# RWKV chunk recurrence in 64x64 quarters of TensorE's array, in a one-core hybrid layer

## The chip, the core and the metric

The kernel runs on one core of a Trainium2 chip. The metric is the device time of one execution in microseconds: the median of the runs shown, lower is better. [...]

## What is computed

One layer of a diffusion backbone over 512 latent tokens and 256 context tokens of width 2048: a modulated RMS norm, one input projection, an mLSTM head group and an RWKV-7 head group, an output projection, and a gated convolutional FFN. The change touches the RWKV group alone: 16 heads of 64 channels, scanned forward and backward, first over the context (from a zero state), then over the latent tokens (from the context's final state).

```python
def rwkv7_scan(r, w, k, v, kk, a, s0, reverse):
    def step(s, xs):
        r_t, w_t, k_t, v_t, kk_t, a_t = xs
        s = (s * w_t[:, :, None, :]
             - jnp.einsum("bhvk,bhk->bhv", s, kk_t)[..., None] * (kk_t * a_t)[:, :, None, :]
             + v_t[..., :, None] * k_t[..., None, :])
        return s, jnp.einsum("bhvk,bhk->bhv", s, r_t)
    ...
y = y_f + y_b
```

## The kernel before

All arithmetic is float32. The large projections split weights and operands in a high and a low part (lines 299 and 300) and make three products of each (lines 370 to 372 and 403 to 405). The RWKV scan is done in chunks of 64 tokens, 4 of context and 8 of latent tokens, for 8 pairs of heads and two directions. A pair and direction is a unit; two heads share the 128 partitions.

- prep makes a unit's operands: scaled keys and receptances KR, scaled b and k in BK, their products G (line 745), masked by VectorE (line 747), and the token-major b and k by transposes (line 756, copied by ScalarE in line 758). All goes to DRAM, to GK_d.
- tsolve inverts the 32x32 diagonal blocks of all chunks, a problem to a partition, in 60 operations of VectorE for a batch (lines 800 and 801), and stores the blocks (803 to 808).
- chain_load loads two chunks of a unit and joins the two inverted blocks to a 64x64 inverse, by eight 32x32 products into the tile ct (lines 834 and 838) and a copy by ScalarE (836) and by VectorE (839).
- chain_step does one chunk of one unit in the PSUM tile R: line 859 multiplies the state M, a block-diagonal [128, 128] of two heads, by the operands; 861 adds the values' part, a head at a time; ScalarE copies (863); 865 applies the inverse; ScalarE copies (866); 868 makes the state's update, 871 adds to y; ScalarE copies y (872); VectorE updates M (876), a head at a time.
- y of each unit is stored to DRAM, and finalize_pair loads both directions' and adds them (924). The state at the context's end goes through DRAM, Mst.

The jobs form a pipeline: operands of job i, inverses of job i - 1, chain of job i - 2 (x_job, ctx_job). In between stand the projections of the latent tokens, and VectorE accumulates late chunks of the modulation (232). A planner, which simulates times of its own, sets each engine's fixed order from the program's order and a few priorities (weight loads are drawn ahead by AHEAD). PSUM has eight banks: two acc, two pre, one ct, three R. SyncE's queue is in order: an issue that waits holds up those behind.

## Time and profile before

| | before |
|---|---|
| median of 3 runs, us | 3351.02 (3346.22 to 3354.89) |
| span of the profiled execution, us | 3344.3 |
| TensorE, VectorE, ScalarE busy | 97%, 63%, 36% |
| instructions | 50011 |
| mean rate of the DMAs | 165 GB/s |

The profile records one execution. An engine's busy time is the time in which it worked on an instruction; matmuls are pipelined and their ends are modelled, so a burst's own pace is read from the starts in order of time. In all views L and a number is a line of the kernel, and a tile is named without its buffer's number. Stages are given in us from the span's start.

### The profile page before, as it was taken

What the parts mean: (1) busy time and instruction counts of PE and PEld (TensorE: products, weight loads), DVE (VectorE), ACT (ScalarE), POOL (GpSimd) and SP (SyncE); (2) the same over time, 40 slices, a digit from 0 to 9 for tenths busy, and PEclk for the clock granted to TensorE, in tenths of its full rate; (3) what the DMA queues carried; (4) which work ended last, traced back from release to release, by engine and by line L of the source; (5) the groups of instructions that cost most, each with busy time, mean ns of one, the idle gap of its engine ahead of it and who ended that gap; (6) DMA issues with size and microseconds to landing.
All of it is one profiled execution on the core that took longest, in us unless ns stands there. A gap on an engine that the chain in (4) does not pass through costs nothing.

```text
span 3344.3 us, 50011 instructions
## 1 busy us (share of the span) xinstructions
PE 3246.0 (97%) x18566; PEld 2610.8 (78%) x18566; DVE 2097.5 (63%) x4010; ACT 1197.9 (36%) x2474; POOL 51.0 (2%) x113
## 2 busy tenths in 40 slices
PE   8999999999999999999998899999999999999998
PEld 5688778787787878777677688888888888888887
DVE  2578777777475776665754787465555555555657
ACT  4356544333334444344323432232222222222323
POOL 0000101000000000000000000000000000000000
PEclk9999999999999999999999999999999999999999
DMA  8878656566567678776764355333333333333332
GB/s 280 306 241 243 185 156 161 162 212 206 187 188 230 194 234 253 207 233 214 260 211 130 99 190 183 95 95 97 96 97 95 95 100 96 95 95 95 101 95 101
DMA packets 391938, 552.97 MB, mean 165 GB/s; under 512 B 131312, under 2 KB 256520, under 8 KB 391440
## 3 DMA queue, kind: packets, MB, share of 16 engines
q1 hardware_dynamic: 382048, 536.41, 51.9%
q10 hardware_dynamic: 9648, 13.37, 1.1%
q8 instruction: 147, 2.41, 0.3%
q14 instruction: 95, 0.78, 0.1%
HBM read 459.06 MB, written 90.61 MB: 164 GB/s over the span
## 4 chain that ended last, share of the span: by engine, by line
PE 82%; DMA 8%; DVE 6%; ACT 2%; issue 1%; SPq 1%; DVEq 0%; ACTq 0%
PE acc L372 12%; PE acc L371 12%; PE acc L370 12%; PE acc L1350 5%; PE acc L1351 5%; PE acc L1352 5%; DMA am<-in_wmod 3%; PE R L859 2%; PE R L861 2%; PE R L865 2%; PE pre L195 2%; PE acc L405 2%; PE acc L404 2%; PE pre L745 2%; PE acc L403 2%
## 5 line engine op out<-in xcount | busy, mean ns | idle before, releaser
L299 ACT CAST whi<-wraw 128x512 fp32r<-128x512 f32 (+1 forms) x948 | 569.7, 604 | 1319.8 <-PE acc L371 715.9
L300 DVE TENSOR_TENSOR wlo<-wraw,whi 128x512 fp32r<-128x512 f32 (+1 forms) x948 | 629.2, 666 | 457.5 <-ACT whi L299 440.6
L370 PE MATMUL acc<-H,whi 128*128 128x512 f32 x1920 | 761.7, 397 | 4.0 <-ACT ev L520 3.0
L372 PE MATMUL acc<-H,wlo 128*128 128x512 f32 x1920 | 761.4, 397 | 3.7 <-DVE wlo L300 3.7
L371 PE MATMUL acc<-H,whi 128*128 128x512 f32 x1920 | 761.1, 396 | 0.0
L372 PEld LDWEIGHTS acc<-H,wlo 128*128 128x128 f32 x1920 | 362.7, 189 | 83.8 <-DVE wlo L300 4.9
L370 PEld LDWEIGHTS acc<-H,whi 128*128 128x128 f32 x1920 | 362.9, 189 | 82.8 <-ACT ev L520 3.2
L371 PEld LDWEIGHTS acc<-H,whi 128*128 128x128 f32 x1920 | 362.8, 189 | 79.2 <-issue 3.6
L1354 DVE SCALAR_TENSOR_TENSOR x<-acc,mod,x 128x512 f32<-128x512 f32 (+1 forms) x192 | 135.6, 706 | 221.9 <-PE acc L1352 221.8
L1298 DVE SCALAR_TENSOR_TENSOR f_cv<-upad,fvec,f_cv 128x512 f32<-128x512 f32 x352 | 263.7, 749 | 7.2
L1350 PE MATMUL acc<-fh,whi 128*128 128x512 f32 x640 | 253.2, 396 | 0.0
L1351 PE MATMUL acc<-fl,whi 128*128 128x512 f32 x640 | 253.1, 396 | 0.0
L1352 PE MATMUL acc<-fh,wlo 128*128 128x512 f32 x640 | 253.1, 396 | 0.0
L232 DVE SCALAR_TENSOR_TENSOR adacc<-am,csil,adacc 128x512 f32<-128x512 f32 x240 | 179.4, 748 | 91.8 <-DMA am<-in_wmod 89.8
L404 PE MATMUL acc<-whi,H 128*128 128x256 f32 x512 | 155.7, 304 | 0.0
L403 PE MATMUL acc<-whi,H 128*128 128x256 f32 x512 | 154.6, 302 | 0.3 <-DVE ev L434 0.3
L405 PE MATMUL acc<-wlo,H 128*128 128x256 f32 x512 | 152.7, 299 | 0.3 <-DVE wlo L300 0.3
L1352 PEld LDWEIGHTS acc<-fh,wlo 128*128 128x128 f32 x640 | 120.2, 188 | 29.1
L1350 PEld LDWEIGHTS acc<-fh,whi 128*128 128x128 f32 x640 | 120.2, 188 | 29.0
L1351 PEld LDWEIGHTS acc<-fl,whi 128*128 128x128 f32 x640 | 120.2, 188 | 29.0
L876 DVE SCALAR_TENSOR_TENSOR r_M<-r_M,r_gC,R 64x64 f32<-64x64 f32 x352 | 98.3, 279 | 48.1 <-ACT r_yt L872 33.0
L1236 PE MATMUL acc<-H,whi 128*128 128x512 f32 x256 | 101.6, 401 | 9.0 <-ACT H L299 7.9
(346 smaller groups left out, 4837.3 us busy)
## 6 DMA issues: line engine op xcount, KB each, us to landing
am<-in_wmod SPq DMA_DIRECT2D x128, 512.0 KB
wraw<-in_wup SPq DMA_DIRECT2D x88, 512.0 KB
wraw<-in_wgate SPq DMA_DIRECT2D x88, 512.0 KB
wraw<-in_wdn SPq DMA_DIRECT2D x88, 512.0 KB
wraw<-in_wcm SPq DMA_DIRECT2D x72, 512.0 KB
r_GK<-GK_d SPq DMA_DIRECT2D x64, 512.0 KB
wraw<-in_wtm SPq DMA_DIRECT2D x56, 512.0 KB
GK_d<-r_Gp SPq DMA_DIRECT2D x32, 512.0 KB
```

What stands on the lines that cost most here:

```text
L299: act.copy(hi, t)
L300: dve.tensor_tensor(lo, t, hi.bitcast(F32), ALU.subtract)
L370: pe.matmul(pt[:, :n], hi(k8), H.h(k), start=k == 0, stop=False)
L371: pe.matmul(pt[:, :n], hi(k8), H.l(k), start=False, stop=False)
L372: pe.matmul(pt[:, :n], lo(k8), H.h(k), start=False, stop=k == KT - 1)
L403: pe.matmul(o, H.h(k)[:, xs], hi(k4), start=first, stop=False, skip_group_check=True)
L404: pe.matmul(o, H.l(k)[:, xs], hi(k4), start=False, stop=False, skip_group_check=True)
L405: pe.matmul(o, H.h(k)[:, xs], lo(k4), start=False, stop=k == KT - 1, skip_group_check=True)
L1298: dve.scalar_tensor_tensor(cv, u[:, a:a + GH, b:b + GW], fvec[:, f, tap:tap + 1], cv, ALU.mult, ALU.add)
L1350: pe.matmul(pt, hi(m)[:, k, :], th[:, cs], start=k == 0, stop=False)
L1351: pe.matmul(pt, hi(m)[:, k, :], tl[:, cs], start=False, stop=False)
L1352: pe.matmul(pt, lo(m)[:, k, :], th[:, cs], start=False, stop=k == GF - 1)
```

## The change

The recurrence holds each head on its own half of the partitions and works in 64x64 quarters of the array: a quarter reads partitions 0 to 63 or 64 to 127 and writes one of the two halves of a PSUM bank. Both directions of a pair are done in one step, in two banks of R, one for each head; a chunk's operands lie in one row of 512 floats (kc = 128 of KR, 2 kc of G, 128 of token-major b and k; 320 in context), in S_d. The backward direction's keys are stored in reversed order, so that both directions' systems are solved in the same form, without the transposed copies. The joins move from chain_load into tsolve, for all chunks of a pair at once, in the PSUM tile pre; the solved and joined rows go back to S_d. The state M, [128, 64] for a unit, stays on chip from context to latent tokens (16 buffers); v is loaded once for a pair; y of both directions is summed on chip by VectorE and stored once for a pair. R gets four banks, ct goes; the finalization's transposes use pre. The mask's table is made to suit. Comments are dropped throughout.

```diff
-    PB = {"acc": 2, "pre": 2, "ct": 1, "R": 3}
+    PB = {"acc": 2, "pre": 2, "R": 4}
...
-            dve.tensor_tensor(KR[:, cc, 0:64], v3(s.kk[:, 0:n]), E1[:, cc, e_prev], ALU.mult)
+            back = slice(None, None, -1) if d else slice(None)
+            dve.tensor_tensor(KR[:, cc, 0:64][:, :, back], v3(s.kk[:, 0:n]), E1[:, cc, e_prev], ALU.mult)
+            dve.scalar_tensor_tensor(BK[:, cc, 0:64][:, :, back], v3(t1)[:, cc], -1.0, v3(E2)[:, cc], ALU.mult, ALU.mult)
             if x:
                 dve.tensor_tensor(KR[:, cc, 64:128], v3(s.r), E1[:, cc, e_cur], ALU.mult)
-        dve.scalar_tensor_tensor(BK[:, :, 0:64], v3(t1), -1.0, v3(E2), ALU.mult, ALU.mult)
         dve.tensor_tensor(BK[:, :, 64:128], v3(kd), v3(E2), ALU.mult)
-        GK_d = DT("GK_d", [P, 2, 8, 256], 16)
-        G_d = GK_d[:, 0].rearrange("p c (h t) -> p c h t", t=128)
-        KB_d = GK_d[:, 1]
-        sp.dma_start(KB_d[:, :, 0:kc], KR[:, :, 0:kc])
-        # G^T[(b|k) s, (kappa|r) t] per chunk and head
+        sp.dma_start(S[:, :, 0:kc], KR[:, :, 0:kc])
         for hf in range(2):
-            G = rp("r_Gp", [P, 4, 2, 128], GPB)
+            G = rp("r_Gp", [P, 4, 2, kc], GPB)
             gd = d if x else hf
             pgs = [PS("pre", [P, 4, 128]) for _ in range(2)]
             for c4 in range(4):
                 for h, pg in enumerate(pgs):
-                    hs = slice(64 * h, 64 * h + 64)
+                    hs = LOHI[h]
                     c = 4 * hf + c4
                     pe.matmul(pg[:, c4, 0:kc], BK[hs, c, :], KR[hs, c, 0:kc], start=True, stop=True)
             for h, pg in enumerate(pgs):
-                dve.tensor_tensor(G[:, :, h, 0:kc], pg[:, :, 0:kc], gmask[:, gd, None, 0:kc].to_broadcast([P, 4, kc]), ALU.mult)
-            sp.dma_start(G_d[:, 4 * hf:4 * hf + 4, :, 0:kc], G[:, :, :, 0:kc])
-        # (b|k) e^(cum_C - cum), token-major, for the state
+                for j, js in enumerate(LOHI):
+                    dve.tensor_tensor(G[LOHI[h], :, j, :], pg[js, :, 0:kc], gmask[js, gd, None, 0:kc].to_broadcast([64, 4, kc]), ALU.mult)
+            sp.dma_start(S[:, 4 * hf:4 * hf + 4, kc:3 * kc], G.rearrange("p c j t -> p c (j t)"))
...
-            act.copy(bt, pb)
-            sp.dma_start(KB_d[:, cs, kc:kc + 128], bt)
+            for h, hs in enumerate(LOHI):
+                for js in LOHI:
+                    act.copy(bt[hs, :, js], pb[js, :, hs])
+            sp.dma_start(S[:, cs, 3 * kc:3 * kc + 128], bt)
...
+    def tsolve(pairs):
+        nc_ = 2 * pairs[0][0].nch
+        n = 4 * nc_ * len(pairs)
+        x = rp("t_X", [P, 32, 32], 1)[0:n]
+        def blocks():
+            q = 0
+            for us in pairs:
+                for r in range(0, P, 32):
+                    o = us[0].kc + r % 64
+                    yield x[q:q + nc_], us[0].S_d[r:r + 32, :, o:o + 32].rearrange("s c t -> c s t")
+                    q += nc_
...
-        dve.tensor_copy(X[half:n], Y[half:n].rearrange("p s t -> p t s"))
...
-        act.copy(Y, x.rearrange("p s t -> p t s"))
-        sp.dma_start(so[0, 0:n], X)
-        sp.dma_start(so[1, 0:n], Y)
-        for u in units:
-            for b in range(2):
-                for ps_, g in blocks(u, b):
-                    sp.dma_start(g, (X if u.d == 0 else Y)[ps_])
+        for t, g in blocks():
+            sp.dma_start(g, t)
+        XT = rp("t_X", [P, 2, 16, 32], 1)
+        for k, us in enumerate(pairs):
+            kc = us[0].kc
+            T_d = us[0].S_d[:, :, kc:kc + 64]
+            T = rp("t_Y", [P, 16, 64], 1)[:, 0:nc_]
+            sp.dma_start(T, T_d)
+            W = XT[:, k, 0:nc_]
+            dve.transpose(W, T[:, :, 0:32])
+            ws = [PS("pre", [P, 16, 32])[:, 0:nc_] for _ in range(2)]
+            a_, b_ = ([slice(64 * h + o, 64 * h + o + 32) for h in range(2)] for o in (0, 32))
+            f = dict(start=True, stop=True, skip_group_check=True)
+            for c in range(nc_):
+                for h, pw in enumerate(ws):
+                    pe.matmul(pw[b_[h], c, :], T[a_[h], c, 32:64], W[a_[h], c, :], **f)
+            for h, pw in enumerate(ws):
+                act.copy(W[b_[h]], pw[b_[h]])
+            for c in range(nc_):
+                for h, pw in enumerate(ws):
+                    pe.matmul(pw[a_[h], c, :], W[b_[h], c, :], T[b_[h], c, 32:64], **f)
+            for h, pw in enumerate(ws):
+                dve.tensor_copy(T[a_[h], :, 32:64], pw[a_[h]])
+            sp.dma_start(T_d, T)
...
+        o = rk("r_GK", [P, 2, 512], 6)[:, :, 0:3 * u.kc + 128]
+        sp.dma_start(o, u.S_d[:, cu:cu + 2, :])
...
+    def chain_v(p, seg, nch):
+        t = rk("r_V", [P, 8, 64], 3)[:, 0:nch]
+        for h, hs in enumerate(LOHI):
+            o = (p % 2) * 128 + 64 * h
+            sp.dma_start(t[hs], v_d[seg][p // 2, :, :, o:o + 64].rearrange("a (b t) v -> t (a b) v", t=64))
+        return t
...
+    def chain_step(us, ops, cs, V, y, first, last):
+        x = us[0].seg == "x"
+        kc = us[0].kc
+        bank = [PS("R", [P, 8, 64]) for _ in range(2)]
+        pos = (0, 1) if cs[0] < cs[1] else (1, 0)
+        opened = {}
+        def mm(h, half, o, w, rhs):
+            hs = LOHI[h]
+            out = bank[h][LOHI[half], o, :]
+            at = opened.get((h, half))
+            f = dict(stop=True, skip_group_check=True)
+            if at is None:
+                opened[(h, half)] = pe.matmul(out, w[hs], rhs[hs], start=True, **f)
+                return
+            with tc.issue_after(at.ins):
+                pe.matmul(out, w[hs], rhs[hs], start=False, **f)
+        w = [o[:, c % 2] for o, c in zip(ops, cs)]
+        kinds = range(2) if x else range(1)
+        for src in range(2):
+            for k, u in enumerate(us):
+                for j in kinds:
+                    for h in range(2):
+                        o = 2 * kc * src + 64 * j
+                        mm(h, h if j == 0 else 1 - h, pos[k], w[k][:, o:o + 64], u.M if src == 0 else V[:, cs[k], :])
+        Rs = rk("r_Rs", [P, 2, 64], 3)
+        U = rk("r_U", [P, 2, 64], 3)
+        for h, hs in enumerate(LOHI):
+            act.copy(Rs[hs], bank[h][hs, 0:2, :])
+        for k, u in enumerate(us):
+            for h in range(2):
+                mm(h, 1 - h, 2 + pos[k], w[k][:, kc:kc + 64], Rs[:, pos[k], :])
+            for h in range(2):
+                if not last:
+                    mm(h, h, 2 + pos[k], w[k][:, 3 * kc + 64:3 * kc + 128], V[:, cs[k], :])
+        for h, hs in enumerate(LOHI):
+            act.copy(U[hs], bank[h][LOHI[1 - h], 2:4, :])
+        for k, u in enumerate(us):
+            for h in range(2):
+                if not last:
+                    mm(h, h, 2 + pos[k], w[k][:, 3 * kc:3 * kc + 64], U[:, pos[k], :])
+            for h in range(2):
+                if x:
+                    mm(h, 1 - h, pos[k], w[k][:, kc + 64:kc + 128], U[:, pos[k], :])
+        if not last:
+            for k, u in enumerate(us):
+                g = u.g0 + cs[k]
+                for h, hs in enumerate(LOHI):
+                    dve.scalar_tensor_tensor(u.M[hs], u.M[hs], u.gC[hs, g:g + 1], bank[h][hs, 2 + pos[k], :], ALU.mult, ALU.add)
         if x:
+            lo, hi = min(cs), max(cs)
+            for h in range(2):
+                hs = LOHI[1 - h]
+                out = y[hs, lo:hi + 1:hi - lo, :]
+                if first:
+                    dve.tensor_copy(out, bank[h][hs, 0:2, :])
+                else:
+                    dve.tensor_tensor(out, bank[h][hs, 0:2, :], out, ALU.add)
+    def chain(pairs, mid):
+        x = pairs[0][0].seg == "x"
+        nch = pairs[0][0].nch
+        Vs, ys = [], []
+        for us in pairs:
+            Vs.append(chain_v(us[0].p, us[0].seg, nch))
+            ys.append(rk("r_yt", [P, 8, 64], 2) if x else None)
+            for u in us:
+                if not x:
+                    Mst[(u.p, u.d)] = rk("r_M", [P, 64], 16)
+                    pool.memset(Mst[(u.p, u.d)], 0.0)
+                u.M = Mst[(u.p, u.d)]
+        n = nch // 2
         for i in range(n):
+            if x and i == 1:
                 mid()
+            ops = [[chain_load(u, i if u.d == 0 else n - 1 - i) for u in us] for us in pairs]
+            for c in range(2 * i, 2 * i + 2):
+                for us, o, V, y in zip(pairs, ops, Vs, ys):
+                    chain_step(us, o, (c, nch - 1 - c), V, y, c < nch // 2, x and c == nch - 1)
+        if x:
+            for us, y in zip(pairs, ys):
+                y_d = us[0].y_d = DT("yr_d", [4, P, 128], 8)
+                for h in range(2):
+                    sp.dma_start(y_d[:, :, 64 * h:64 * h + 64].rearrange("a (b t) v -> t (a b) v", t=64), y[LOHI[1 - h]])
...
-        for t, u in ((y, uf), (sq, ub)):
-            sp.dma_start(t, u.y_d.rearrange("a p v -> p a v"))
+        sp.dma_start(y, uf.y_d.rearrange("a p v -> p a v"))
         g4 = lambda t: t.rearrange("p a (h c) -> p (a h) c", h=2)
         b8 = lambda t: t[:, :, None].to_broadcast([P, 8, 64])
-        dve.tensor_tensor(y, y, sq, ALU.add)
```

## Rows read from the trace of the kernel before

**Rows 1.** The page: span, busy time by engine, chain that ended last.
```profile
span 3344.3 us, 50011 instructions
...
PE 3246.0 (97%) x18566; PEld 2610.8 (78%) x18566; DVE 2097.5 (63%) x4010; ACT 1197.9 (36%) x2474; POOL 51.0 (2%) x113
...
PE 82%; DMA 8%; DVE 6%; ACT 2%; issue 1%; SPq 1%; DVEq 0%; ACTq 0%
```
**Rows 2.** Busy time by stage: busy us (instructions) by engine, granted clock, DMA share, GB/s.
```profile
400.00:1650.00 1250.00, 1222.26 (x8721) 964.31 (x8722) 836.70 (x1911) 503.47 (x1252) 27.97 (x71) 0.97 0.69 206
200.00:400.00 200.00, 186.75 (x1258) 166.16 (x1256) 167.28 (x325) 122.37 (x209) 20.19 (x19) 0.98 0.73 220
500.00:600.00 100.00, 99.17 (x810) 78.79 (x809) 74.76 (x196) 41.05 (x98) 9.98 (x11) 0.98 0.58 159
```
**Rows 3.** The same view, from 400 to 1650 us, for tile R, then ct.
```profile
400.00:1650.00 1250.00, 353.56 (x2782) 263.31 (x2782) 98.27 (x352) 127.27 (x512) 0.97 0.69 206
...
400.00:1650.00 1250.00, 91.22 (x1560) 66.63 (x1560) 31.38 (x102) 24.35 (x96) 0.97 0.69 206
```
**Rows 4.** TensorE in order of time (start, length, line, shapes, count): chunks' bursts.
```profile
1012.61 0.49 PE L859 MATMUL R<-r_M,r_GK 128*128 128x128 f32 x2
1012.93 0.39 PE L868 MATMUL R<-r_UV,r_GK 128*128 128x128 f32 x2
1013.25 0.45 PE L871 MATMUL R<-r_UV,r_GK 128*64 128x64 f32 x4
1013.63 0.44 PE L861 MATMUL R<-r_UV,r_GK 64*64 64x64 f32 x4
1014.00 0.71 PE L745 MATMUL pre<-r_KR,r_BK 64*128 64x128 f32 x4
```
**Rows 5.** The same view: the dense stream, a burst of the recurrence, the stream again.
```profile
1015.22 0.28 PE L404 MATMUL acc<-whi,H 128*128 128x256 f32 x1
1015.33 0.28 PE L405 MATMUL acc<-wlo,H 128*128 128x256 f32 x1
1015.54 0.45 PE L871 MATMUL R<-r_UV,r_GK 128*64 128x64 f32 x4
1015.92 0.39 PE L403 MATMUL acc<-whi,H 128*128 128x256 f32 x1
1016.14 0.28 PE L404 MATMUL acc<-whi,H 128*128 128x256 f32 x1
```
**Rows 6.** The same view: two lines of different row halves, and a join.
```profile
1333.84 0.27 PE L861 MATMUL R<-r_UV,r_GK 64*64 64x64 f32 x1
1333.85 0.27 PE L865 MATMUL R<-r_Rs,r_GK 64*64 64x64 f32 x1
...
1334.00 0.22 PE L861 MATMUL R<-r_UV,r_GK 64*64 64x64 f32 x1
1334.01 0.22 PE L865 MATMUL R<-r_Rs,r_GK 64*64 64x64 f32 x1
1334.06 0.22 PE L861 MATMUL R<-r_UV,r_GK 64*64 64x64 f32 x1
1334.07 0.22 PE L865 MATMUL R<-r_Rs,r_GK 64*64 64x64 f32 x1
1334.22 0.43 PE L834 MATMUL ct<-t_XT,r_GK 32*32 32x32 f32 x8
1334.58 0.38 PE L403 MATMUL acc<-whi,H 128*128 128x256 f32 x1
```
**Rows 7.** The same view: the modulation's product in four column blocks.
```profile
25.62 0.64 PE L195 MATMUL pre<-H,r_kr 128*32 128x256 f32 x8 [1.27 <-DVE sq L258]
```
**Rows 8.** Groups of instructions, VectorE (busy us, mean ns | idle before).
```profile
L747 DVE TENSOR_TENSOR r_Gp<-pre,c_gmask 128x512 f32<-128x512 f32 x64 | 42.7, 687 | 16.5 <-PE pre L745 14.8 <-PE acc L404 1.1
...
L839 DVE COPY r_GK<-ct 32x128 f32<-32x128 f32 x96 | 26.9, 280 | 34.1 <-PE ct L838 26.2 <-issue 3.0 <-ACT whi L299 2.5
```
**Rows 9.** The chain that ended last, longest pieces from 800 to 1300 us.
```profile
798.03 4.40 DMA GK_d<-r_sg
```

More of the change, by code (lines that the diff above doesn't have):

```diff
@@ L647, in body @@
     la = {}
-    Mst = DT("Mst", [NPAIR, 2, P, P])
+    Mst = {}
+    LOHI = (slice(0, 64), slice(64, 128))
     v_d = {"c": DT("v_c", [4, 2, P, 256]), "x": DT("v_x", [4, 4, P, 256])}
@@ L801, in tsolve @@
             dve.tensor_tensor(x[:, 0:t, t + 1:32], x[:, 0:t, t + 1:32], w, ALU.add)
-        act.copy(Y, x.rearrange("p s t -> p t s"))
-        sp.dma_start(so[0, 0:n], X)
-        sp.dma_start(so[1, 0:n], Y)
-        for u in units:
-            for b in range(2):
-                for ps_, g in blocks(u, b):
-                    sp.dma_start(g, (X if u.d == 0 else Y)[ps_])
+        for t, g in blocks():
+            sp.dma_start(g, t)
[21 more added lines that the diff above has]
+            sp.dma_start(T_d, T)
@@ L833, in chain_load @@
-        for i in range(4):
-            pe.matmul(pw[fb, 32 * i:32 * i + 32], o.G[fa, i // 2, i % 2, fb], XT[fa, i, :], start=True, stop=True)
-        ws = XT.rearrange("s a t -> s (a t)")
-        act.copy(ws[fb], pw[fb, 0:128])
-        for i in range(4):
-            pe.matmul(px[fa, 32 * i:32 * i + 32], ws[fb, 32 * i:32 * i + 32], o.G[fb, i // 2, i % 2, fb], start=True, stop=True)
-        dve.tensor_copy(o.G[fa, :, :, fb], px[fa].rearrange("p (c h t) -> p c h t", h=2, t=32))
-        return o
@@ L842, in chain_init @@
-    def chain_init(u):
-        u.M = rk(f"r_M{u.d}", [P, P], 4)
-        if u.seg == "c":
-            pool.memset(u.M, 0.0)
-        else:
-            sp.dma_start(u.M, Mst[u.p, u.d])
-            u.y_d = DT("yr_d", [4, P, 128], 16)
-    def chain_step(u, o, c, last):
-        x = u.seg == "x"
-        kc = 128 if x else 64
-        ci = c % 2
-        UV = o.UV[:, ci, :]
-        bank = PS("R", [P, 4, P])
-        pR, pU, pM = (bank[:, i, :] for i in range(3))
-        pU = pU[0:64]
-        H2 = [slice(64 * h, 64 * h + 64) for h in range(2)]
-        pe.matmul(pR[0:kc], o.KB[:, ci, 0:kc], u.M, start=True, stop=False, skip_group_check=True)
-        for h, hs in enumerate(H2):
-            pe.matmul(pR[0:64, hs], o.G[64:128, ci, h, 0:64], UV[64:128, hs], start=False, stop=True, skip_group_check=True)
-        Rs = rk("r_Rs", [64, P], 2)
-        act.copy(Rs, pR[0:64])
-        for h, hs in enumerate(H2):
-            pe.matmul(pU[:, hs], o.G[0:64, ci, h, 0:64], Rs[:, hs], start=False, stop=True, skip_group_check=True)
-        act.copy(UV[0:64], pU)
-        if not (x and last):
-            pe.matmul(pM, o.KB[:, ci, kc:kc + 128], UV, start=not x, stop=True, skip_group_check=True)
-        if x:
-            for h, hs in enumerate(H2):
-                pe.matmul(pR[64:128, hs], o.G[:, ci, h, 64:128], UV[:, hs], start=False, stop=True, skip_group_check=True)
-            act.copy(o.y[64 * ci:64 * ci + 64], pR[64:128])
-            if last:
-                return
-        for hs in H2:
-            dve.scalar_tensor_tensor(u.M[hs, hs], u.M[hs, hs], u.gC[hs, u.c0 + c:u.c0 + c + 1], pM[hs, hs], ALU.mult, ALU.add)
-        if last:
-            sp.dma_start(Mst[u.p, u.d], u.M)
@@ L880, in chain @@
-    def chain(us, mid):
-        for u in us:
-            chain_init(u)
-        n = us[0].nch // 2
+        o = rk("r_GK", [P, 2, 512], 6)[:, :, 0:3 * u.kc + 128]
+        sp.dma_start(o, u.S_d[:, cu:cu + 2, :])
+        return o
+    def chain_v(p, seg, nch):
[4 more added lines that the diff above has]
+        return t
@@ L885, in chain @@
+    def chain(pairs, mid):
[11 more added lines that the diff above has]
+        n = nch // 2
         for i in range(n):
-            if us[0].seg == "x" and i == 1:
+            if x and i == 1:
@@ L943, in finalize_pair @@
         yield
-        pt = PS("ct", [P, 512])
+        pt = PS("pre", [P, 512])
         for tt in range(4):
@@ L1110, in do_chain @@
             job = [t for _ in range(n) for t in chain_q.pop(0)]
-            chain([u for _, us, _ in job for u in us], fin_step)
+            chain([us for _, us, _ in job], fin_step)
             fin_q.extend(t for t in job if t[2] is not None)
@@ L1116, in do_solve @@
             jobs = [solve_q.pop(0) for _ in range(n)]
-            tsolve([u for job in jobs for _, us, _ in job for u in us])
+            tsolve([us for job in jobs for _, us, _ in job])
             chain_q.extend(jobs)
@@ L1124, in ctx_job @@
             s = pair_shared(pp, "c")
-            job.append((pp, prep(pp, s, "c"), None))
+            job.append((pp, prep(pp, s, "c", DT("Sc_d", [P, 8, 320], 8)), None))
         do_solve()
@@ L1441, in pack @@
     gm = np.zeros((P, 2, P), f)
-    s_ = (idx % 64)[:, None]
-    t_ = (idx % 64)[None]
-    strict = idx[None] < 64
-    gm[:, 0] = np.where(strict, s_ < t_, s_ <= t_)
-    gm[:, 1] = np.where(strict, s_ > t_, s_ >= t_)
+    isb, strict = (idx < 64)[:, None], (idx < 64)[None]
+    for d in range(2):
+        s_, t_ = ((np.where((idx < 64) & (d == 1), 63 - idx % 64, idx % 64)) for _ in range(2))
+        s_, t_ = s_[:, None], t_[None]
+        if d:
+            s_, t_ = -s_, -t_
+        gm[:, d] = np.where(strict, s_ < t_, s_ <= t_)
     o["gmask"] = gm
```

62 lines of the change are left out of this document (8 added, 54 removed).

## Prediction

> **What bounds the kernel now.** I read the page's first lines, then the busy time by stage, then the instructions in order of time. The page [rows 1] shows TensorE busy for 97% of the span and the chain that ended last 82% on it, so TensorE time that is freed can shorten the kernel, until another engine is late. The change lies in one stage, from about 400 to 1650 us, in which the RWKV chunks run between the projections. There TensorE is busy 1222 of 1250 us, VectorE 837, ScalarE 503, the DMA engines 69% [rows 2]. The recurrence writes one tile, R, the joins of the inverses another, ct: they hold 354 and 91 us of TensorE's busy time there [rows 3], 445 together. The reader should see that they are a good third of a stage in which TensorE has nearly no idle time, at a granted clock of 0.97, so mostly at the upper of its two levels.
>
> What do those 445 us consist of? In order of time [rows 4], one chunk of one direction is five short bursts, each followed by another form: L859 takes 0.32 us to the next start, L868 0.32, L871 0.38, L861 0.37, and L865, of the same form as L861, the same 0.37. A burst of L861 is two 64x64 products, and the row counts four: a float32 product is two instructions. Going from a dense stream into such a burst and back costs more: within the stream a 256-column product starts 0.11 to 0.12 us after the last one, but L871 starts 0.21 after L405, and the second product after the return comes 0.22 after the first [rows 5]. That is 0.09 in and 0.11 out, 0.20 a round trip.
>
> So before: 1.77 us for each of 128 latent unit-chunks (8 pairs, 2 directions, 8 chunks) is 227 us; a context one lacks L871, 1.39 for 64 of them, 89 us. Each stops twice for ScalarE's copies, so I count two round trips: 384 at 0.20 is 77. A join is two bursts of eight 32x32 instructions, 0.36 us each [rows 6], 192 bursts, 69 us, with a round trip for every second one, 19. In all 481, against the 445 that the view gives without the way in; I take 465.
>
> **The change part by part.** *The quarters.* They make more instructions, not fewer. A latent step of a pair (both directions) has 32 products, 64 instructions, for the 16 products of two unit-chunks before; a context step 20 for 12. That is 3968 + 1280 in the recurrence (the last step of each latent pair lacks 16) where there were 2782 [rows 3]; the joins keep 1536. The gain can only come from instructions that run at once in different quarters. The trace has such a case: where L861 (rows 64 to 127) and L865 (rows 0 to 63) are adjacent, they alternate, L865 starts 0.01 us behind L861, and each further round of two costs 0.06; eight instructions are through in 0.38 us [rows 6], as long as four of one position [rows 4]. Column positions do it too: eight instructions of four column blocks end after 0.64 us [rows 7], and one after another they would need eight times the 0.11 of a 256-column stream [rows 5] and a latency on top, over 0.9. No row shows rows and columns divided at once; this is the first unknown. Its ends: four quarters at once, or two.
>
> A piece of four rounds costs 0.38 + 0.20 = 0.58, each further round 0.06. A latent pair step stops twice, so three pieces; with four quarters at once they have 8, 4 and 4 rounds: 0.82 + 0.58 + 0.58 = 1.98, times 64 is 127 us. A context step also comes to 8, 4 and 4 (its first piece uses two quarters only): 63 us for 32. With two at once: 16, 8, 8 and 8, 8, 4 rounds, 2.94 and 2.22, 188 and 71 us. The joins become 32 pieces (two a pair and segment) of 64 or 32 instructions in two positions at once, so 32 or 16 rounds of 0.03 (an eighth of a burst, less its change): about 1.28 and 0.80 with the way in and out, 33 us. TensorE then needs 223 or 292 us for what took 465: it frees 242 or 173. I take 205.
>
> The Trainium skill (TensorEngine Tiling (Array Packing), section Key Properties) says that changing the tiling mode drains TensorE. The round trip of 0.20 us agrees, and as the change goes from five forms a unit-chunk to one form a piece, this speaks for it; were it free, the round trips, 96 us before and 64 after, would take 32 us off the gain.
>
> *VectorE.* Here the change adds. The mask on G was one operation a head and half on all partitions; now each is two on 64 partitions with the same 512 elements, and a row of this kind takes 0.687 us [rows 8]: 64 more in the latent part, 44 us, and in context 32 more at half the length, some 11. The sum of y moves from ScalarE's 128 copies to 128 operations of VectorE from PSUM, between the 0.28 of a small copy and the 0.69 of a full one [rows 8]; they have 128 elements, so I take 0.30, 38 us. The joins' copies fall from 96 at 0.28, 27 us, to 32 of 512 or 256 elements, 17 us, with 16 block transposes that no row shows: 0.28 to 1.4 each (twice a full operation), I take 0.5, 8 us. The sum of two y's in the finalization goes, 8 of 0.69, 5 us. Net about 85: VectorE has some 920 us of work in this stage. TensorE alone would let the stage shrink from 1250 to 1045 us, where VectorE would have to be busy 88% of the time. The highest share that a stage shows is 167 of 200 us, 84% [rows 2]; at 84%, 920 us need about 1100. So VectorE, with its fixed order, takes over as the limit, and of the 205 us some 150 are left.
>
> *ScalarE* loses the copies of y and of the joins and the transposed copies of the solve, and gets each copy of the token-major b and k in four pieces. At 40% [rows 2] I cost that at nothing: TensorE's other work hides it. Without that cover (VectorE's split waits for ScalarE's) it would be counted in the recurrence, two more waits of a pair step.
>
> *Solve and queues.* The solve now stores its blocks, loads whole rows back, joins, stores again, and only then can the chunks be loaded. A DMA of such a tile is on the chain with 4.40 us [rows 9]. Two pairs share one buffer, so they follow each other: two transfers and some 4 us of work each, 25 to 28 us a solve. Seven solves have a job of other work behind them; the last stands right ahead of the last chain, so I charge it once, 25 us; covered it costs nothing, uncovered at all eight 200. While SyncE waits there for the stores, the weight loads and those of the modulation stand behind it in the queue, and TensorE's products wait for these; against this, some 260 issues of DMAs go (64 of v, 96 of the inverses' corners, 48 of y, 32 of the state and others, less 32 new ones). The joins now take both banks named pre while they run, which the preparation also uses; R has four banks for two pair steps, where three held three unit steps.
>
> Sum: 150 - 25 = 125 us off the profiled execution's 3344.3 [rows 1]: 3219. Its median is 3351.02, 6.7 above that span; I add this for what lies around it: 3226.
>
> **The rivals.** *The cover holds:* VectorE keeps up at a share of 88%, since what it waits for now is mostly TensorE's pace, and the solve is hidden. The whole 173 to 242 comes through: 3110 to 3178, some 3146. For it: ScalarE and DMA have room; against it: no stage shows that share.
>
> *VectorE is late early:* if the stage holds VectorE busy no more than the 75% of a dense slice now [rows 2], 920 us need 1227 and only some 24 us are left: 3327. For it: VectorE's queue is in order and stands behind the modulation's transfers; against it: it was TensorE that set the pace in that slice, at 99%.
>
> *The quarters do not run at once* (the change then does not do what it says): each instruction costs 0.06 us. Pieces of 32, 16 and 16 rounds cost 4.9 us, of 16, 16 and 8 rounds 3.4; 311 + 109, and the joins 56: 476 us, 11 more than now, and 25 for the last solve: 3387, slower. The point from which it decides: the sum breaks even where an instruction of the 6784 takes about 0.053 us on average, (465 less 108 for changes and ways in) / 6784. For it: the densest stretch that I find, 16 small instructions [rows 6], needs about 0.05 each, and nothing before issues more in a row; against it: the alternating eight at 0.03. The Trainium skill (TensorE: Matmul & The Clock Gate, Part 1) names a floor of about 25 ns from start to start, and about 62 ns for a matmul where the sequencer's software decodes it. The starts 0.01 us apart contradict neither as averages; by 62 ns the time would be, as an estimate from that page with the sum above (6784 of them and 108 us, against 465, and 25 for the solve), about 90 us above that of before; at 25 ns the forecast stands.
>
> **How the numbers follow.** Forecast (VectorE takes over at 84%) 0.44, around 3226, with its own range 3185 to 3275; the cover holds 0.22; VectorE late early 0.16; no overlap 0.18. For two in ten left out, the range goes from 3130 to 3345: it takes in the two-quarter and four-quarter ends and the 75% case, and leaves out the slower one. A measurement of this kernel tells about 0.3%, 10 us, from no change. Within that: the outer part of the 75% case and the inner part of the last, 0.07. Faster 0.77, slower 0.16.
>
> **What would show each step.** Right: in the order of time, products of R start in groups of four within 0.05 us, a new group each 0.06; the tile R holds under 300 us of TensorE in its stage, with about 5250 instructions; VectorE's share there is over 80%; the mask's 192 operations still take 0.69 and 0.42. Wrong: instructions of R at an even 0.06 (no overlap); TensorE idle in the stage while VectorE is at 75%; long waits ahead of the loads of r_GK for the solve's stores. The forecast falls if the bursts are cut up by the projections into more than three pieces a step, since each costs 0.34 us before its first extra round.

## The result, and the profile after

| | before | after |
|---|---|---|
| median, us (lowest to highest) | 3352.78 (3346.22 to 3354.89) | 3582.53 (3581.2 to 3588.28) |
| span of the profiled execution, us | 3344.3 | 3586.5 |

The ratio of the times is 1.0695, with an interval from 1.0676 to 1.0715: the change makes the kernel 230 us slower, where 125 us less were forecast. The page of the kernel after, against [rows 1] (span, busy time by engine; then busy tenths of TensorE and its granted clock in 40 slices of 90 us; then the chain that ended last):

```profile
span 3586.5 us, 54671 instructions
...
PE 3149.9 (88%) x21030; PEld 2553.9 (71%) x21030; DVE 2181.3 (61%) x4178; ACT 1212.4 (34%) x2427; POOL 52.7 (1%) x113
...
PE   8999899999999844716659889999999999999998
PEclk9999999999999855556779999999999999999999
...
PE 46%; DMA 10%; DVE 7%; ACT 2%; issue 1%; SPq 1%; DVEq 0%; ACTq 0%
```

TensorE is busy for 96 us less than before, though it issues more instructions; the span is 242 us longer. The lost time shows between 1200 and 1900 us, where TensorE is often idle and its granted clock lies between half, the lower of its two levels, and three quarters. But the preparations, which follow each other in a row, are late before that, while projections still fill TensorE. Its sign is the first product of each pair's preparation, two instructions a pair (length min/median/max in ns, first and last start in us); of the kernel after, all eight pairs:

```profile
L669 PE MATMUL pre<-r_t,c_bones x16: 589/1060/1222, 653.8 to 1481.6; 128*128 128x512 f32 x16
```

That is 118 us a step, 116 over the last seven pairs. The kernel before makes a step in 93 us (the last seven pairs, 670.8 to 1226.6; shown with the experiments). The last preparation begins 255 us later than before, and the span is 242 us longer. Busy time by stage of the kernel after (as [rows 2]), then the tile R alone (as [rows 3]):

```profile
1200.00:1300.00 100.00, 69.04 (x871) 54.12 (x869) 64.91 (x148) 32.62 (x88) 4.80 (x5) 0.62 0.60 177
1300.00:1400.00 100.00, 26.61 (x382) 21.93 (x382) 48.45 (x107) 13.55 (x27) 0.71 (x3) 0.51 0.39 108
1400.00:1500.00 100.00, 69.20 (x936) 55.13 (x938) 68.45 (x160) 37.84 (x95) 1.47 (x6) 0.55 0.56 176
1500.00:1600.00 100.00, 30.30 (x212) 24.01 (x208) 62.67 (x139) 16.71 (x43) 0.78 (x3) 0.50 0.47 135
```

```profile
400.00:1900.00 1500.00, 211.23 (x5248) 174.20 (x5248) 123.26 (x480) 99.03 (x384) 0.80 0.58 176
```

So the recurrence itself did what was hoped: 5248 instructions hold 211 us of TensorE where 2782 held 354. No engine is near its limit in the slices of loss. What TensorE waited for, 1200 to 1700 us of the kernel after (line and releaser: us, times, longest), and the chain there in order of time (start, length):

```profile
PE pre L816 <- DVE t_X L810: 121.1, 4, 49.7
PE pre L747 <- DVE r_BK L736: 23.5, 5, 8.7
```

```profile
1366.71 4.39 DMA t_Y<-Sx_d
1371.38 0.72 DVE t_X L810
1372.19 1.94 PE pre L816 x64
...
1379.29 4.05 DMA Sx_d<-t_Y
1383.53 4.43 DMA t_Y<-Sx_d
1387.98 0.72 DVE t_X L810
1388.80 1.92 PE pre L816 x64
...
1391.78 2.09 PE pre L821 x63
1393.87 0.68 DVE t_Y L823
1394.59 2.09 PE pre L669 x2
```

L816 is the first product of the joins. TensorE stands up to 49.7 us ahead of it, while VectorE solves (60 operations, 1325 to 1361 us, between those of the modulation), the blocks go to DRAM and come back. With VectorE's copy of the last join (L823) comes L669, the first product of the next preparation. It writes the tile pre too, and both banks of that name belonged to the joins, which stand ahead of it in the program. It is so for every second pair, since two pairs share a solve.

### The profile page after: what moved, and what is told of

It is laid out like the page before. It is cut to its first block, busy times and chain, and to the rows that moved or that the text cites. A ratio compares the mean times of both kernels' runs of the same rounds, so it can differ in the third digit from the quotient of the medians.

```text
span 3586.5 us, 54671 instructions
## 1 busy us (share of the span) xinstructions
PE 3149.9 (88%) x21030; PEld 2553.9 (71%) x21030; DVE 2181.3 (61%) x4178; ACT 1212.4 (34%) x2427; POOL 52.7 (1%) x113
## 4 chain that ended last, share of the span: by engine, by line
PE 46%; DMA 10%; DVE 7%; ACT 2%; issue 1%; SPq 1%; DVEq 0%; ACTq 0%
PE acc L372 9%; PE acc L370 9%; PE acc L371 9%; PE acc L1376 4%; PE acc L1378 4%; PE acc L1377 4%; DMA am<-in_wmod 3%; DVE adacc L232 2%; PE acc L1262 1%; PE acc L1263 1%; PE acc L1264 1%; PE pre L621 1%; DMA x_d<-ev 1%; DMA Sx_d<-r_Gp 1%; DMA Sx_d<-r_sg 1%
## 5 line engine op out<-in xcount | busy, mean ns | idle before, releaser
L403 PE MATMUL acc<-whi,H 128*128 128x256 f32 x512 | 150.3, 295 | 0.3 <-ACT whi L299 0.3
L404 PE MATMUL acc<-whi,H 128*128 128x256 f32 x512 | 150.1, 294 | 0.0
L750 DVE TENSOR_TENSOR r_Gp<-pre,c_gmask 64x512 f32<-64x512 f32 (+1 forms) x192 | 115.0, 599 | 40.4 <-DMA Sx_d<-r_Gp 24.0
```

The lines of the kernel that those rows point to most:

```text
L403: pe.matmul(o, H.h(k)[:, xs], hi(k4), start=first, stop=False, skip_group_check=True)
```

## The experiments

Ratios are to the kernel before, run beside it on the same chip, with a 95% interval. Four theories. A: the banks named pre tie the next preparation to the end of the solve. B: the solve's longer way through DRAM, by itself. C: the projections ran out early, and the rest ran at half clock. D: the row of preparations, solves and the last chain sets the length of the stage, and TensorE is full only because the planner fills it.

**Banks (e1, e2).** One line of the kernel after; and the tie put into the kernel before, at the end of tsolve.

```diff
 e1, after:
-            ws = [PS("pre", [P, 16, 32])[:, 0:nc_] for _ in range(2)]
+            ws = [PS("R", [P, 16, 32])[:, 0:nc_] for _ in range(2)]
 e2, before:
+        hold = [PS("pre", [32, 32]) for _ in range(2)]
+        for pt in hold:
+            pe.matmul(pt, X[:, 0, :], X[:, 31, :], start=True, stop=True)
+        for i, pt in enumerate(hold):
+            act.copy(T1[0:32, 32 * i:32 * i + 32], pt)
```

> The changed kernel, with the joins of the inverses in the tile R in place of pre, nothing else. Theory A (the joins take both pre banks in the program's order, so the preparation of the next pair, which needs pre, waits until the solve is through): the preparation of the fifth pair starts beside the solve of the third and fourth instead of behind its joins, the period of two pairs falls from some 237 us to some 160, TensorE's waits for the solve's transposes go, and the time falls to 3200 to 3330. Theory B (the solve's longer way through DRAM holds the chain, whatever bank the joins use): the period stays, 3550 to 3600. Theory C (the planner pulled the projections ahead and the rest runs at half clock): the projections still end near 1230 us, 3500 or more.

Measured: 3366.59 us, 1.0066 [1.0040, 1.0092]. By the ratios some 210 us come back, with the way through DRAM and the quarters unchanged; it is still above the 3330 that theory A allowed. The first products of all eight pairs in e1:

```profile
L669 PE MATMUL pre<-r_t,c_bones x16: 590/592/697, 561.0 to 1265.7; 128*128 128x512 f32 x16
```

The last preparation begins 216 us earlier than in the kernel after.

> The kernel before, with two small products at the end of each solve that take both pre banks (32x32 each, read by nobody), so that the preparation behind it has to wait for the solve, and nothing else. Theory A: the preparation no longer overlaps the solve; the eight solves of some 50 to 90 us each stand partly bare, and the time grows by 60 to 200 us, 3410 to 3550. Theories B and C: two products of half a microsecond a solve change nothing that can be measured, 3345 to 3360.

Measured: 3465.59 us, 1.0368 [1.0335, 1.0401]: two small products in these banks after the solve, with ScalarE's two copies of them, cost the kernel before 120 us. Its last seven pairs take 679 us from first to last, where they took 556:

```profile
L668 PE MATMUL pre<-r_t,c_bones x14: 590/592/697, 681.7 to 1361.1; 128*128 128x512 f32 x14
```

So A is shown from both sides, and B is not what cost the 210 us; nor is C by itself: from 1200 to 1300 us the granted clock is 0.62 in the kernel after and 0.96 in e1, with the tie gone. Later e1 is at a lower clock too, 0.75 on the mean from 1300 to 1700 us (two rows of e1):

```profile
1200.00:1300.00 100.00, 92.08 (x1084) 75.69 (x1087) 77.15 (x153) 46.80 (x98) 2.28 (x4) 0.96 0.84 259
1300.00:1700.00 400.00, 273.80 (x2671) 210.44 (x2672) 240.30 (x576) 111.66 (x318) 2.12 (x11) 0.75 0.64 202
```

TensorE's waits for the solve, 700 to 1700 us, at e2's two products and then at e1's joins (us, times, longest):

```profile
PE pre L811 <- DVE t_X L801: 33.0, 1, 33.0
```

```profile
PE R L816 <- DVE t_X L810: 25.1, 3, 11.2
```

The 49.7 us of the kernel after are 11.2 at most with the tie gone. But of the 125 us nothing is there. That was the second question.

**Engines (e3, e4, e17, e18).** e3 leaves one of three products out of the latent projections of pairs and heads in the kernel before; e4 leaves out every second accumulation of the late modulation in e1. e18 does both in the kernel before, and e17 in e7 (below), in both with the loads of what is left out.

```diff
 e3:
-                pe.matmul(pt[:, :n], hi(k8), H.l(k), start=False, stop=False)
+                if not thin[0]:
+                    pe.matmul(pt[:, :n], hi(k8), H.l(k), start=False, stop=False)
 e4:
-            else:
+            elif k % 2 == 0 or after is not None:
                 dve.scalar_tensor_tensor(acc, wm[:, k % 2], csil[:, k:k + 1], acc, ALU.mult, ALU.add)
```

> The kernel before, with one of the three products (high weights by low operand) left out of the latent tokens' projections for the pairs and the heads; splits, loads and all else stay, so TensorE alone gets some 170 us less work in the stage from 750 to 1600 us. The prediction's step (TensorE's time in this stage is the kernel's time, until VectorE is at 84%): 3200 to 3270. Theory D (the stage's length is set by the row of preparations, solves and mLSTM heads, which go through VectorE and ScalarE; TensorE is full because the planner fills it with projections that could come later): under 60 us, 3290 to 3350.

Measured: 3360.36 us, 1.0048 [1.0032, 1.0063].

> As e1 (joins in R), and in the late chunks of the modulation ahead of the FFN every second accumulation on VectorE is left out (its operand is still loaded; the modulation is then not that of the reference): 96 operations of 0.75 us less, 72 us of VectorE's work between 750 and 1700 us. Theory D with VectorE as the pace: 30 to 90 us less than e1's 3367, 3280 to 3335. If the pace is set by waits for DMAs and the order of the steps alone, under 15 us: 3352 to 3370. If TensorE's time sets it, no change.

Measured: 3357.88 us, 1.0028 [1.0010, 1.0045], some 9 us less than e1.

> The kernel of e7 with two parts left out at once: the product of the weights' high part with the low part of the normalised x in the latent projections of pairs and heads (as e3, some 170 us of TensorE), and every second load and accumulation of the late modulation before the FFN (some 72 us of VectorE and 24 MB of transfers); the output is not the reference's. If the engines together set the stage, each taking over where another is relieved: 3200 to 3290 us, 60 to 150 less than e7. If the row of preparations, solves and the last chain sets it: within 30 us of e7, 3322 to 3382 us, with TensorE idle and its granted clock low in most of 700 to 1700 us.

Measured: 3351.31 us, 1.0014 [0.9994, 1.0034]; e7 has 1.0011.

> The kernel before with the same two parts left out. Engines together: 3190 to 3290 us. The row: within 30 us of before, 3315 to 3375 us. If this one gains and e17 does not, the row is longer in the changed kernel and the engines set the kernel before.

Measured: 3354.94 us, 1.0038 [1.0014, 1.0061]. Leaving out some 170 us of TensorE (by my estimate: 512 instructions at 0.22 us from start to start and 512 at 0.11 to 0.12), 72 us of VectorE and 24 MB of loads brings nothing, in either kernel. TensorE's busy time itself falls by 64 us in e3, 68 in e18 and 105 in e17, since many of the products that are left run at a lower clock. The preparations come no closer together. Below are their first products, seven pairs each, of the kernel before, e18, e7 and e17, and then the busy time from 700 to 1300 us of e18 and e17:

```profile
L668 PE MATMUL pre<-r_t,c_bones x14: 591/592/1201, 670.8 to 1226.6; 128*128 128x512 f32 x14
```

```profile
L674 PE MATMUL pre<-r_t,c_bones x14: 590/634/1222, 697.4 to 1265.2; 128*128 128x512 f32 x14
```

```profile
L672 PE MATMUL pre<-r_t,c_bones x14: 590/592/1201, 676.2 to 1248.3; 128*128 128x512 f32 x14
```

```profile
L678 PE MATMUL pre<-r_t,c_bones x14: 592/697/1220, 681.3 to 1265.9; 128*128 128x512 f32 x14
```

```profile
700.00:1300.00 600.00, 571.96 (x3908) 449.65 (x3907) 390.73 (x849) 251.22 (x590) 23.30 (x31) 0.85 0.66 203
```

```profile
700.00:1300.00 600.00, 469.25 (x5563) 378.09 (x5567) 456.08 (x1027) 241.65 (x563) 16.68 (x29) 0.78 0.66 201
```

From the first of these pairs to the last it is 556, 568, 572 and 585 us, six steps of 93 to 97 us. In e17 TensorE is busy 78% of this stretch, VectorE 76%, and the steps are the longest. For the changed kernel that speaks for D. For the kernel before one other reading is left: in e18 TensorE is still busy 572 of 600 us, part of it at a lower clock (0.85 on the mean), so what its relief gave went into projections drawn ahead and then into slower products. Which of the two held e18 back is argued, not shown.

**The modulation's loads (e5 to e8).** In e1 thirty loads of 512 KB through one buffer follow each other from 1383 to 1570 us, most of them on its chain. Theory S: they set the end; theory P is D by another name.

```diff
 e5 (e1) and e6 (before):
-            if k % 2 == 0:
+            if k % 2 == 0 and (after is not None or k % 4 == 0):
                 wm = am() if after is None else fp("am", [P, 2, 512], 2)
 e7 (e1) and e8 (before):
-        return sm("am", [P, 2, 512], 1)
+        return sm("am", [P, 512], 2)
...
+                one = am()
+                sp.dma_start(one, A["wmod"][j, k // 2, :, k % 2])
```

> The kernel of e1 with every second load of the late modulation (512 KB each, 48 of 96) left out, each load now serving four accumulations; VectorE's work is as in e1, the output is not the reference's. In e1's chain of waits 30 such loads stand one behind the other between 1383 and 1570 us, each 3.1 to 6.1 us and ahead of one or two accumulations of 0.75 us, because they share one buffer. Theory S (this stream of loads through one buffer sets the end of the stage once the solves are free): 15 loads of about 4.2 us leave that stretch, so 3290 to 3320 us, with TensorE busier than 50 and 67 of 100 us in 1400 to 1600. Theory P (the row of preparations, solves and the last chain sets it): within 15 us of e1, 3350 to 3380.

> The kernel before with the same 48 loads left out. Theory S: if the stream sets the stage there too, 40 to 70 us less, 3280 to 3310 us. Theory P: within 15 us of before. If e5 gains and this one does not, the stream became the bound only with the change.

Measured: 3366.74 us, 1.0061 [1.0034, 1.0088], and 3349.44 us, 0.9997 [0.9973, 1.0021]. S falls: the loads form a chain of waits through one buffer, and half of them can go without a gain.

> The kernel of e1 with the same bytes of late modulation, loaded as 256 KB into two buffers of 512 columns instead of 512 KB into one of two times 512: a load can run beside the accumulation of the one before, at twice the number of loads. Nothing is left out. Theory S: in 1383 to 1570 us the accumulations (about 0.75 us, 45 of them, 34 us) go beside loads, so 20 to 45 us less than e1: 3320 to 3345 us. Theory P: within 15 us of e1.

> The kernel before with the late modulation in two buffers in the same way; nothing left out. Theory S: 15 to 40 us less than before, 3305 to 3330 us. Theory P, or S with a stream that binds only in e1: within 15 us of before, 3335 to 3365.

Measured: 3352.44 us, 1.0011 [0.9995, 1.0027], and 3378.98 us, 1.0079 [1.0055, 1.0103]. e7 is some 15 us faster than e1 and the fastest form of the change that leaves nothing out; it draws with the kernel before, and no form beat it. As e8 loses 26 us with the same edit, and e5 gained nothing, I don't credit the buffers with these 15: another order from the planner may do as much. e8's 3378.98 us lie above both of its ranges.

**The preparation made longer (e11, e12).** The running sum goes to DRAM and back on GpSimd's queue, in each of the 16 preparations of x.

```diff
+            if x:
+                way = DT("way_d", [P, NX], 2)
+                pool.dma_start(way, cum)
+                pool.dma_start(cum, way)
```

> The kernel before with each of the 16 preparations of x made longer without work for an engine: the running sum r_cum goes to DRAM and back before it is used, two transfers of about 4.4 us on a queue of their own (GpSimd's), some 9 to 10 us. Twelve of the preparations lie in the stage. If the row of preparations sets the stage in the kernel before: 80 to 150 us more, 3430 to 3500 us. If TensorE's work sets it and the preparations have room: within 25 us of before, below 3375 us.

> The kernel of e7 with the same detour in each of the 16 preparations. Row of preparations: 80 to 150 us more than e7, 3432 to 3502 us. Engines' work (TensorE or VectorE) sets the stage: within 25 us of e7, below 3377 us. If the kernel before has room and this one has none, the change moved the bound from TensorE to the preparations.

Measured: 3418.9 us, 1.0221 [1.0186, 1.0256], and 3434.1 us, 1.0262 [1.0235, 1.0288], that is 69 us more than before and some 82 more than e7. The transfers took less than I had thought (median us from issue to landing, kernel before with the detour):

```profile
way_d<-r_cum POOLq DMA_DIRECT2D x16, 256.0 KB, 2.9
r_cum<-way_d POOLq DMA_DIRECT2D x16, 256.0 KB, 3.8
```

So 6.7 us each, 107 for sixteen, 80 for the twelve between the first and the last of the seven pairs. The first products of these pairs, e11 and then e12:

```profile
L668 PE MATMUL pre<-r_t,c_bones x14: 590/592/1201, 676.2 to 1259.1; 128*128 128x512 f32 x14
```

```profile
L672 PE MATMUL pre<-r_t,c_bones x14: 591/594/1220, 679.1 to 1314.1; 128*128 128x512 f32 x14
```

In e12 the row grows by 63 us (635 against 572), most of 80; in e11 by 27 (583 against 556). In e11 the last preparation begins 32 us later than before and the profiled span is 70 us longer, so that more than half of its loss comes after that. Its time lies between its two ranges, that of e12 at the lower end of the row's. Delay in a preparation costs time where relief of the engines brings none. In the changed kernel the row has little room; in the kernel before more of each delay is covered while the preparations run.

**Single ties of the preparation (e9, e10, e13 to e16).** The half-pair's serial work passes through single buffers. e9 (on e7) and e10 (on before) put the half that leaves last into r_t instead of r_sg; e13 does so within a pair only; e14 moves one bank from R to pre; e15 does both; e16 loads ScalarE's table for Ln and Exp ahead of the pair's Ln.

```diff
 e9, e10:
-            bt = rp("r_sg", [P, 4, 128])
+            bt = rp(("r_sg", "r_t1")[hf], [P, 4, 128])
 e13:
+            bt = rp("r_t1" if x and d == 0 and hf else "r_sg", [P, 4, 128])
 e14:
+    PB = {"acc": 2, "pre": 3, "R": 3}
 e16:
+        ln_exp()
         act.activation(sq[:, :n], pn[:, :n], AF.Ln, bias=BK12)
```

> The kernel of e7 (banks of R for the joins, two buffers for the modulation) with one tie inside the preparation loosened: the second half of the transposed tile goes into the buffer r_t instead of r_sg, which holds the first half and is also the first thing that the next preparation writes. In e7 ScalarE waited 32.2 us at the copies into r_sg and 15.5 us at the next preparation's first write of r_sg, both for the transfer of r_sg to DRAM, in 700 to 1300 us, over some 13 preparations. Theory P (the preparations stand one behind the other, and the length of one sets the stage): most of these 48 us leave the row, so 20 to 45 us less than e7, 3307 to 3335 us. If an engine sets the stage instead (TensorE 88 to 97, VectorE 71 to 89 of 100 us there): within 10 us of e7, 3342 to 3363 us.

> The kernel before with the same tie loosened. The waits for the transfer of r_sg are 8.6 and 14.0 us in 700 to 1300 us there. Theory P for the kernel before too: 10 to 23 us less, 3325 to 3337 us. TensorE's work (97% busy) sets it: within 10 us of before.

Measured: 3439.18 us, 1.0275 [1.0252, 1.0298], and 3416.84 us, 1.0217 [1.0188, 1.0246]. Both miss, with the other sign. ScalarE now waits for r_t's transfer, which the next pair's preparation needs first: in e9 23.2 us in six waits from 690 to 1300 us, but in e10 only 4.5 in two. Most of the loss is older: the first latent pair's first product starts at 621.6 us in e9 against 559.3 in e7, and at 610.4 in e10 against 559.4 before. That is 62 and 51 us of some 87 and 67, lost by the time the context's part is through, to which the edit applies too. e13, which leaves the context and the next pair alone, is some 4 us behind e7. So a tie was moved, and not loosened; which of its waits costs the context's time was not followed further.

> The kernel of e7 with the second half of the transposed tile in r_t only for the forward direction of a pair of x, so that the backward direction can begin before that half has left, and nothing is tied to the next pair or in the context (in e9 ScalarE waited 23.2 us in 690 to 1300 us for the transfer of r_t ahead of the next pair's square, and the context's part was already 63 us late at its end). If the tile sets the length of a preparation: 3 to 6 us for each of 6 pairs in the stage, 3316 to 3336 us. If it does not: within 10 us of e7, 3342 to 3362 us.

> The kernel of e7 with three banks of PSUM named pre instead of two, and three named R instead of four. If the banks named pre set the length of a preparation (every product of it passes through two): the next half's products start beside the mask of the one before, 2 to 4 us for each of 24 halves in the stage, 50 to 90 us less than e7, 3262 to 3302 us. If the chain of R, now with three banks for two pair steps, is late instead: 20 to 80 us more than e7. If neither: within 15 us.

> Both of e13 and e14. If each loosens a tie of its own, the gains add; if one tie hides the other, this one is faster than the better of the two by more than their sum: 3240 to 3300 us. If R's third bank sets it: as e14, slower than e7.

> The kernel of e7 with one set of ScalarE's tables that holds Ln and Exp loaded ahead of the pair's Ln: of the table loads that stand in each pair's chain (two of 1.28 us between the square's sum and its root) one goes. Chain of the preparation: 1.3 us for each of 16 pairs, some 8 in the stage, 8 to 20 us less than e7, 3332 to 3344 us. Otherwise: within 6 us of e7.

Measured: 3356.34 us, 1.0031 [1.0012, 1.0049]; 3373.04 us, 1.0085 [1.0056, 1.0115]; 3375.03 us, 1.0084 [1.0054, 1.0114]; 3369.04 us, 1.0070 [1.0048, 1.0093]. None gains in time. e16 did not save a load: its trace still has two table loads a pair from 700 to 1150 us, one ahead of the sum of squares and one at the tanh behind the root (57 in all, 51 in e7). In e14 and e15 the preparations do come faster at first. Below are the first products of the first five pairs, e7 and then e15; the last three pairs of e15; and e15's sixth pair in order of time:

```profile
L672 PE MATMUL pre<-r_t,c_bones x10: 591/594/1201, 559.3 to 947.7; 128*128 128x512 f32 x10
```

```profile
L672 PE MATMUL pre<-r_t,c_bones x10: 592/594/766, 544.3 to 847.5; 128*128 128x512 f32 x10
L672 PE MATMUL pre<-r_t,c_bones x6: 592/595/1220, 1102.6 to 1297.7; 128*128 128x512 f32 x6
```

```profile
904.57 0.63 ACT L670 ACTIVATE r_t<-r_kk 128x512 f32<-128x512 f32 x1
...
1102.20 0.60 PE L974 MATMUL pre<-c_ident,r_y 128*128 128x128 f32 x4
1102.64 1.02 PE L672 MATMUL pre<-r_t,c_bones 128*128 128x512 f32 x2
```

Four steps take 303 us in e15 and 388 in e7; then the sixth pair comes 255 us after the fifth. Its operand r_t is ready 197 us before its first product, and what stands right ahead of that product in pre is the finalization's transposes (L974), which the change moved from ct to pre. It is the same in e14 (136 us), and twice in e7. So the finalization may be a second tie through these banks, of the kind that e1 took away. No run takes it off them; TensorE had other work meanwhile (246 of 250 us from 850 to 1100 us of e15), so what this is worth is not shown. What sets the 95 us a pair, and how much the planner's new order gives or takes in each of these, stays open.

## Why the prediction was wrong

**The failed step: solve and queues.** It says itself that the joins "take both banks named pre while they run, which the preparation also uses", and gives that no price. It asked how long the way from solve to chain is, and charged that once, as the other seven solves "have a job of other work behind them". The question left out was who else needs these banks. In program order the joins stand ahead of the next preparation, at every second pair, so this one began only after the solve and both pairs' joins; before, it ran beside the solve. The profile could have shown it: preparations follow each other every 93 us (six steps between 670.8 and 1226.6), the solve's 60 operations lie beside them (927 to 1016 us one solve, 933 us the start of the next preparation), and a tie turns that into a sum. Its price is some 210 us by e1 and 120 in the kernel before by e2. The length of the way itself was sized some 10 us too short: from VectorE's last solve operation at 1361 us it is 33 us to the copy of the last join at 1394, and 38 until the chain's load behind the last store is issued at 1399, against 25 to 28.

**The first step: "TensorE time that is freed can shorten the kernel".** This fails for the changed kernel, and the runs give no support for it in the kernel before. Where a planner draws projections into every gap, the 97% of [rows 1] does not tell what TensorE's time is worth: e3 left out products worth some 170 us and gained nothing. With the tie gone (e1, e7) the projections are through earlier, and TensorE is then idle while the last preparation, solve and chain run: this row is the busy time of e7 from 1300 to 1700 us, and the one below it that of the kernel before.

```profile
1300.00:1700.00 400.00, 279.03 (x2740) 213.02 (x2739) 241.45 (x582) 109.74 (x322) 2.27 (x11) 0.76 0.64 198
```

```profile
1300.00:1700.00 400.00, 386.98 (x2572) 305.94 (x2573) 258.56 (x594) 157.42 (x446) 2.02 (x9) 0.98 0.74 231
```

279 us of 400 against 387, at a granted clock of 0.76 against 0.98: much of the freed time went there.

**The quarters: right, and better than sized.** One piece of 32 instructions of the kernel after, in order of time (start, length, shapes, count), as [rows 6]:

```profile
980.82 0.46 PE L859 MATMUL R<-r_U,r_GK 64*64 64x64 f32 x16
981.10 0.23 PE L859 MATMUL R<-r_V,r_GK 64*64 64x64 f32 x2
981.11 0.23 PE L859 MATMUL R<-r_Rs,r_GK 64*64 64x64 f32 x2
981.16 0.23 PE L859 MATMUL R<-r_V,r_GK 64*64 64x64 f32 x2
981.17 0.23 PE L859 MATMUL R<-r_Rs,r_GK 64*64 64x64 f32 x2
```

Sixteen instructions are through in 0.28 us and a further four start every 0.06 us, as the end with four quarters at once assumed; the rival without overlap is dead. From start to start that is 15 to 18 ns on average, below the 25 that the prediction named as a floor. The tile R holds 211 us (under 300 was asked for) with 5248 instructions (5250). The joins' two lines hold 43 us, part of it at the lower clock, where 33 were said.

**VectorE: the rows right, the limit wrong.** The mask's operations take 0.688 and 0.421 us, as said; y's 128 take 0.289 (0.30), the joins' transposes 0.71 and 0.45 (0.5), their copies 0.68 and 0.41. But the largest share was no limit at 84%: e17 holds VectorE busy 89.88 us of 100 in one slice. Nor did it set the time: e4 took 72 us from it for 9. In the kernel after it was at 48 to 68% from 1200 to 1600 us, where time was lost.

**The rivals.** Two asked how far VectorE follows and one whether the quarters overlap; none had a buffer as its mechanism. The text named the sign that would prove it wrong, "TensorE idle in the stage while VectorE is at 75%", and "long waits ahead of the loads of r_GK for the solve's stores". The first came, with VectorE lower still; the wait stood one step earlier, ahead of the joins. The range had its upper end at 3345, as if nothing could be late but an engine; the chance for a slower kernel, 0.16, stood on quarters that do not overlap.

## What to carry to other kernels

When a step takes over a buffer or a bank that another job uses, write down who stands behind it in program order and what that one ran beside until now; that overlap is the price, not the length of the step. Where a planner fills an engine's queue, a busy share of 97% does not say that this engine sets the time: look at the cadence of the serial row, and ask what it waits for. Test it in both directions, with work left out and with delay put in, before designing for the engine. And when one shared bank is set free, look for the next job that was moved into it.

## What the runs showed of the hardware

Idle TensorE cost twice. Where waits for the solve left it busy for 27 and 30 us of 100, the granted clock was 0.51 and 0.50, its lower level, and it was still 0.55 in the slice between, with 69 us busy. Products are then slower as well: the preparation's first product has a median of 1060 ns in the kernel after and of 592 ns in the kernel before, in the rows above. So the small work that is left after a gap, the preparation's and the chain's, takes longer itself, and a tie that makes TensorE wait also stretches the row that it ties.

The busy share alone does not tell the level. In e3, from 1100 to 1400 us, TensorE was busy for 97, 92 and 82 of each 100 us at a granted clock of 0.61, 0.57 and 0.50, so mostly at the lower level, where the same work fills more of its time:

```profile
1100.00:1200.00 100.00, 97.06 (x630) 75.74 (x626) 69.69 (x162) 32.21 (x96) 1.36 (x5) 0.61 0.63 188
1200.00:1300.00 100.00, 92.16 (x560) 68.68 (x558) 61.21 (x134) 38.37 (x97) 0.67 (x4) 0.57 0.70 210
1300.00:1400.00 100.00, 82.22 (x497) 64.44 (x496) 55.72 (x142) 29.20 (x91) 0.46 (x3) 0.50 0.54 158
```
